# Three of four memory projections moved from behind a branch to the start of the kernel

## The chip, the cores and the metric

The kernel runs on one core of a Trainium2 chip. The metric is the device time of one launch in microseconds (us), the median of the timed runs. The engines named here are TensorE (PE in the profile, with PEld for its weight loads), VectorE (DVE), ScalarE (ACT), GpSimd (POOL) and SyncE (SP), whose queue issues most loads.

## The reference

Two transformer blocks run one after the other on 256 tokens of width 2048, in float32. The parts that matter here:

```
h  = concat(meta_tokens, x)                  # 16 + 256 rows
xn = rms_norm(h, norm1_g); proj = xn @ w_in  # first block, its first step
...
h  = h + peer(rms_norm(h))                   # experts: gelu(u_i . x), then sum of w_i * v_i over chosen i
h  = rms_norm(h, normf_g)
# second block: deltanet branch beside attention over a memory of 256 rows
mem_n = rms_norm(mem, mem_norm_g)
kv = mem_n @ w_kv                            # 2048 x 2048: 1024 columns of keys, 1024 of values
k  = rms_norm(heads of kv[:, :1024], kn_g);  v = kv[:, 1024:]
xa = softmax(q . k / 16) @ v                 # 4 heads of 256
```

The memory, its weights and its gains are inputs. `kv` depends on nothing that the first block computes; its keys and values are used in the second block's attention.

## The kernel before

**Products.** All large products are done in split float32: each operand is written as hi + lo (`split_store`, lines 173 to 180: one ACT operation for hi, one on DVE for lo), and `mm3` issues three matmuls. Weights come in loads of 1 MB into one of four `raw` buffers (SP's queue), are split in two halves into one of four `hi`/`lo` buffers, and are multiplied at once. `proj_a` makes 256 rows by 512 columns of an output out of 2048 inputs: four loads, eight halves, 96 matmuls of 512 columns. `Background` (`bg`) holds generators of small work; each load's `tick` lets one of them go on by its rate, so that this work stands in program order among the matmuls.

**Order.** Up to line 906 the order of every engine's instructions is planned by the compiler's scheduler, which takes the earliest in program order among those that its model has ready. From there on (`manual_schedule`) TensorE's order is the program's; the other engines' is still planned. Each engine then runs its own list strictly in order, with semaphores between them.

**The opening.** SP loads `meta` and the two halves of `x` (1 MB each), then eight rows of gains (`prows`), then the weights of `w_in`. ACT sums squares, DVE makes the rates (`rstd_of`, `rsqrt`: 13 small operations), `along` spreads them over the tokens with TensorE, and 16 sets of transposes (three each, line 335) with `xs` and a split on DVE and ACT make `xh`, `xl`. Then the projections of `w_in` follow.

**The memory.** While the experts' first layer runs (`hidden`, 64 steps), `memory()` loads `mem_T` (2 MB) and `mem_2` (2 MB) in the background from step 30 on, splits the memory with its gain into `mh`, `ml` (16 splits), and makes the rates `mr` of its rows.

**The branch.** The experts that any token chose are listed on the chip. If there are more than 106 x 128 of them, a slower path inside `tc.If` does the work; with these inputs it is not taken. The branch is a point at which all engines meet, and the scheduler moves nothing across it. Behind it stand, in program order: `weigh` for five pairs of rows (four POOL gathers each, two of `gq` and two of `hq`, with two buffers each; DVE multiplies them, and the product is split into `wh`, `wl`, of which the pool `wt` holds seven), the four memory projections (keys, keys, values, values), the transposes of the normalised keys, and the stores of keys and values to `kmd` and `vmd` in DRAM on ACT's queue.

**The value stage.** 53 pairs of rows: for each row of 128 experts, one POOL gather brings 1 MB of value rows into `raw`, it is split, and `add_row` adds it with 24 matmuls into eight PSUM banks. The weights of a pair are fetched five pairs ahead in program order. The last `LP` = 6 pairs are done by halves of the columns, so that the norm of the first half (`norm3(0)`, nine steps) can go beside the second half's matmuls.

Of the kernel before, what the change touches and what calls it, by code (L numbers as in the profile page):

```python
# [74 lines left out]
def _build(tc, nc, V, S, T, G, ctx, I, out):  # L75
# [27 lines left out]
    WA, LP = 5, 6  # L103
# [3 lines left out]

    pn1 = ctx.enter_context(ExitStack())
    nw1 = pn1.enter_context(pool("norm1"))
    meta = nw1.tile([NM, D], F32, name="meta", bufs=1)  # L110
    nc.sync.dma_start(meta, I["meta_tokens"])
    h = hp.tile([128, 2, D], F32, name="h")
    for t in range(2):
        nc.sync.dma_start(h[:, t], I["x"][0, t * 128:(t + 1) * 128, :])

# [111 lines left out]
    def proj_a(w, r0, nk, c0, xh, xl, t0=0):  # L227

        a = [acc() for _ in range(2)]
        for kg in range(nk // 4):  # L230
            src = w[r0 + kg * 512:r0 + (kg + 1) * 512, c0:c0 + 512].rearrange("(k p) n -> p k n", p=128)
            for k0, hi, lo in stream(src, 4, 512):
# [94 lines left out]

    w_in = I["w_in"][0]
    xh, xl = x_tiles(NM + NT)
    toks = [(meta, NM, 0), (h[:, 0], 128, NM), (h[:, 1], 128, NM + 128)]  # L330
    rB = along(nw1, rstd_of(square_sums(toks, nw1.tile([128, D], F32, name="junk")), D, [128, 3]), toks)
    for k in range(KT):
        p = (acc, ptp, acc, pmm)[k % 4]()
        for x, n, o in toks:
            T.transpose(p[:, o:o + n], chunk(x, k), ident[:n, :n])
        xs = nw1.tile([128, NM + NT], F32, name="xs", bufs=3)
        V.tensor_mul(xs, p[:, :NM + NT], rB)
        split_store(xh[:, k], xl[:, k], xs, pcol(N1, k))
# [547 lines left out]

    kmd = tc.dram_tile([128, 8, 256], F32, name="kmd")
    vmd = tc.dram_tile([128, 2, 1024], F32, name="vmd")
    def memory():

        ss = me.tile([128, 2, 4], F32, name="ssq")
        for hf in range(2):
            raw = load(I["mem_T"][:, hf * 8:hf * 8 + 8], [8, NT])
            for k in range(8):
                split_store(mh[:, hf * 8 + k], ml[:, hf * 8 + k], raw[:, k], pcol(MG, hf * 8 + k))
                yield
        for t in range(2):
            x = load(I["mem_2"][0, t * 128:(t + 1) * 128, :], [D])
            for q in range(4):
                S.activation(acc(), x[:, q * 512:(q + 1) * 512], AF.Square, accum_out=ss[:, t, q:q + 1])  # L900
            yield
        s1 = me.tile([128, 2], F32, name="ssr")
        V.tensor_reduce(s1, ss, axis=AX.X, op=OP.add)
        V.tensor_copy(mr, rstd_of(s1, D, [128, 2]))
        yield
# [868 lines left out]
```

## Time and profile before

| | |
|---|---|
| timed runs | 3509.72 us median of 3 (3509.1 to 3510.99) |
| the profiled execution | 3497.31 us, span 3495.4 us, granted clock 0.996 |
| PE busy | 3426.1 us, 98% of the span |
| DVE, ACT, POOL busy | 2386.8, 1626.7, 1031.5 us |
| DMA | 662.30 MB, 189 GB/s over the span |

A time in the timeline counts from the span's start. An engine's idle time in a stretch is the stretch less its busy time. In a timeline row, the brackets give how long the engine stood idle before the instruction and what released it. SPq and ACTq are the queues on which these engines issue DMAs. The opening is the stretch from 0 to about 28 us, the branch lies at about 1913 to 1919 us, the memory projections behind it go on to about 2024 us, and the value stage from there to about 2620 us.

### The profile page before, as it was taken

The page shows a single profiled execution, that of the slowest core. Times are in us where ns is not written, and L with a number is a line of the kernel's source. Part 1 is how long each engine was busy: PE and PEld are TensorE (multiplying, and loading weights), DVE is VectorE, ACT ScalarE, POOL GpSimd, SP SyncE. Part 2 cuts the span into 40 slices and gives each one's busy share as a digit, 9 for nine tenths or more (in the row PEclk, how much of TensorE's full clock was granted, in tenths as well). Part 3 has the DMA queues.
Part 4 walks back from the last instruction along what each step waited for, and adds up shares of the span by engine and source line. Part 5 has one row for each costly group of instructions (what it writes and reads, how often), then busy time and mean ns, then how long its engine had stood idle before and what let it go on. Part 6 is the DMA issues. An engine that isn't in the chain of part 4 may idle for free. (4 is left out here: it accounts for less than half of the span.)

```text
span 3495.4 us, 54464 instructions
## 1 busy us (share of the span) xinstructions
PE 3426.1 (98%) x21754; PEld 3080.0 (88%) x21754; DVE 2386.8 (68%) x4376; ACT 1626.7 (47%) x2148; POOL 1031.5 (30%) x660
## 2 busy tenths in 40 slices
PE   8999999999999999999998999999999999999999
PEld 7988899888889999999998788877778899999987
DVE  6975569977658997666453655544457788888775
ACT  6444443446455444444443544443347545444443
POOL 0000000000003888888810556666620000000000
PEclk9999999999999999999999999999999999999999
DMA  5544445667675676778764877666665444454443
GB/s 164 169 148 142 145 133 176 214 217 257 224 237 173 180 205 191 208 210 241 205 206 140 283 255 242 238 216 216 217 204 173 145 150 152 161 166 152 156 157 109
DMA packets 347976, 662.30 MB, mean 189 GB/s; under 512 B 56047, under 2 KB 205781, under 8 KB 318002
## 3 DMA queue, kind: packets, MB, share of 16 engines
q1 hardware_dynamic: 256962, 472.68, 40.5%
q0 software_dynamic: 71328, 165.08, 16.5%
q10 hardware_dynamic: 19424, 20.98, 1.7%
q8 instruction: 173, 2.83, 0.3%
q14 instruction: 89, 0.73, 0.1%
HBM read 620.47 MB, written 38.19 MB: 188 GB/s over the span
## 5 line engine op out<-in xcount | busy, mean ns | idle before, releaser
L176 ACT CAST hi<-raw 128x1024 fp32r<-128x1024 f32 x1093 | 1145.3, 1049 | 1549.9 <-PE acc L208 532.1
L177 DVE TENSOR_TENSOR lo<-raw,hi 128x1024 fp32r<-128x1024 f32 x1093 | 1330.4, 1222 | 711.7 <-ACT hi L176 706.3
L839 POOL DMA_INDIRECT table<-gts,idx x256 | 573.7, 2241 | 134.1 <-issue 75.3
L206 PE MATMUL acc<-xh,hi 128*128 128x256 f32 (+1 forms) x2048 | 604.2, 295 | 0.7 <-DVE hg L431 0.7
L206 PE MATMUL mm<-xh,hi 128*128 128x256 f32 x2064 | 586.2, 284 | 0.8 <-DVE fit L1017 0.8
L208 PE MATMUL acc<-xh,lo 128*128 128x256 f32 (+1 forms) x2048 | 586.1, 286 | 0.0
L207 PE MATMUL acc<-xl,hi 128*128 128x256 f32 (+1 forms) x2048 | 585.7, 286 | 0.0
L207 PE MATMUL mm<-xl,hi 128*128 128x256 f32 x2064 | 583.9, 283 | 0.0
L208 PE MATMUL mm<-xh,lo 128*128 128x256 f32 x2064 | 583.8, 283 | 0.0
L206 PEld LDWEIGHTS mm<-xh,hi 128*128 128x128 f32 x2064 | 394.9, 191 | 0.9 <-issue 0.8
L207 PEld LDWEIGHTS mm<-xl,hi 128*128 128x128 f32 x2064 | 395.0, 191 | 0.1
L208 PEld LDWEIGHTS mm<-xh,lo 128*128 128x128 f32 x2064 | 394.9, 191 | 0.0
L206 PEld LDWEIGHTS acc<-xh,hi 128*128 128x128 f32 x2048 | 389.7, 190 | 5.4 <-issue 4.9
L207 PEld LDWEIGHTS acc<-xl,hi 128*128 128x128 f32 x2048 | 390.0, 190 | 1.4 <-issue 1.0
L208 PEld LDWEIGHTS acc<-xh,lo 128*128 128x128 f32 x2048 | 389.1, 190 | 1.3 <-issue 1.2
L350 POOL DMA_DIRECT2D table<-zero x16 | 18.0, 1126 | 953.0 <-DVE zero L348 953.0
L206 PE MATMUL acc<-hi,xh 128*128 128x512 f32 x704 | 280.3, 409 | 0.0
L207 PE MATMUL acc<-lo,xh 128*128 128x512 f32 x704 | 278.2, 395 | 0.0
L208 PE MATMUL acc<-hi,xl 128*128 128x512 f32 x704 | 277.7, 394 | 0.0
L739 POOL DMA_INDIRECT gq<-table,ig x106 | 148.9, 1405 | 268.2 <-SPq L1137 153.1
L440 DVE SCALAR_TENSOR_TENSOR h<-hg,cw,h 128x256 f32<-128x256 f32 x480 | 203.4, 478 | 0.0
L207 PE MATMUL acc<-lo,wh 128*128 128x512 f32 x424 | 167.7, 395 | 16.9 <-DVE lo L177 16.9
(547 smaller groups left out, 5630.0 us busy)
## 6 DMA issues: line engine op xcount, KB each, us to landing
raw<-in_peer_u_dram SPq DMA_DIRECT2D x128, 1024.0 KB, 5.1
raw<-in_w_in_dram SPq DMA_DIRECT2D x112, 1024.0 KB, 5.0
raw<-in_dn_w_in_dram SPq DMA_DIRECT2D x88, 1024.0 KB, 4.9
raw<-in_w_out_dram SPq DMA_DIRECT2D x48, 1024.0 KB, 5.0
raw<-in_w_gla_out_dram SPq DMA_DIRECT2D x16, 1024.0 KB, 4.9
table<-zero POOLq DMA_DIRECT2D x16, 1024.0 KB
raw<-in_w_conv_out_dram SPq DMA_DIRECT2D x16, 1024.0 KB, 4.9
raw<-in_peer_wq_dram SPq DMA_DIRECT2D x16, 1024.0 KB, 5.3
```

The lines of the kernel that those rows point to most:

```text
L176: S.copy(hi, src)
L177: V.tensor_sub(lo, src, hi)
L206: T.matmul(o, lhsT=lh, rhs=rh, start=start, stop=False)
L207: T.matmul(o, lhsT=lh, rhs=rl, start=False, stop=False)
L208: T.matmul(o, lhsT=ll, rhs=rh, start=False, stop=stop)
L350: nc.gpsimd.dma_start(table[:128 * 128 * NT].rearrange("(q p a b) o -> q p a (b o)", q=16, p=128, b=128)[q], z[:, None, :].to_broadcast([1 ...
L440: V.scalar_tensor_tensor(ca[:, f], hg[:, f - f0, j:j + NT], w, ca[:, f], op0=OP.mult, op1=OP.add)
L739: G.indirect_dma_start(out=dst, out_offset=None, in_=rows, in_offset=bass.IndirectOffsetOnAxis(ap=ids.bitcast(U32), axis=0))
L839: d = G.indirect_dma_start(out=table, out_offset=bass.IndirectOffsetOnAxis(ap=idx[:, i, s:s + 1].bitcast(U32), axis=0), in_=gts[:, i, s:s ...
```

## The change

- `memory()` moves up in the program and runs twice: at the opening, at once and not in the background, with its own tiles, and, as before, beside the experts' first layer. A hook in it places the loads of `meta` and `x` behind the second load of `mem_T`.
- The first norm becomes a generator, `norm1()`, in the background of three memory projections at the rate 1.6; its transposes use the banks of `ptp` and `pmm` by turns.
- These three projections, the keys of column block 1 and both blocks of values, now stand before the projections of `w_in`. The transposes of the keys of block 1 come between the two of values.
- Behind the branch the keys of block 0 are left, and their transposes follow at once. Their first 512 rows of weights are loaded and split before the branch, into tiles of their own (`begun`).
- `mem_keys` stores the transposed keys in two parts with one buffer (`kms`), where there was one part.
- The pool `wt` has six buffers instead of seven, `LP` is 5 instead of 6, and `norm3(0)` goes on at 1.4 instead of 1.0 a tick.

```diff
-    WA, LP = 5, 6
+    WA, LP = 5, 5
...
+    h = hp.tile([128, 2, D], F32, name="h")
     pn1 = ctx.enter_context(ExitStack())
     nw1 = pn1.enter_context(pool("norm1"))
     meta = nw1.tile([NM, D], F32, name="meta", bufs=1)
-    nc.sync.dma_start(meta, I["meta_tokens"])
-    h = hp.tile([128, 2, D], F32, name="h")
-    for t in range(2):
-        nc.sync.dma_start(h[:, t], I["x"][0, t * 128:(t + 1) * 128, :])
...
-    def proj_a(w, r0, nk, c0, xh, xl, t0=0):
+    def proj_a(w, r0, nk, c0, xh, xl, t0=0, begun=None):
...
-            for k0, hi, lo in stream(src, 4, 512):
+            for k0, hi, lo in begun if begun and kg == 0 else stream(src, 4, 512):
...
+    def memory(hook=None):
+        ss = me.tile([128, 2, 4], F32, name="ssq")
+        for hf in range(2):
+            raw = load(I["mem_T"][:, hf * 8:hf * 8 + 8], [8, NT])
+            if hook is not None:
+                hook(hf)
+            for k in range(8):
+                split_store(mh[:, hf * 8 + k], ml[:, hf * 8 + k], raw[:, k], pcol(MG, hf * 8 + k))
+                yield
...
-    rB = along(nw1, rstd_of(square_sums(toks, nw1.tile([128, D], F32, name="junk")), D, [128, 3]), toks)
-    for k in range(KT):
-        p = (acc, ptp, acc, pmm)[k % 4]()
...
+    def norm1():
+        rs = rstd_of(square_sums(toks, nw1.tile([128, D], F32, name="junk")), D, [128, 3])
+        yield
+        rB = along(nw1, rs, toks)
+        yield
+        for k in range(KT):
+            p = (ptp, pmm)[k % 2]()
+            for x, n, o in toks:
+                T.transpose(p[:, o:o + n], chunk(x, k), ident[:n, :n])
+            xs = nw1.tile([128, NM + NT], F32, name="xs", bufs=3)
+            V.tensor_mul(xs, p[:, :NM + NT], rB)
+            split_store(xh[:, k], xl[:, k], xs, pcol(N1, k))
+            yield
+
+    def first_loads(hf):
+        if hf == 0:
+            return
+        nc.sync.dma_start(meta, I["meta_tokens"])
+        for t in range(2):
+            nc.sync.dma_start(h[:, t], I["x"][0, t * 128:(t + 1) * 128, :])
+
+    def mem_keys(wk, cb, mh, ml, mr, begun=None):
+        ks = []
+        for t, a in enumerate(proj_a(wkv, 0, KT, cb * 512, mh, ml, begun=begun)):
+            ks.append(wk.tile([128, 512], F32, name="kn", bufs=2))
+            heads_norm(wk, a, ks[-1], mr[:, t:t + 1])
+        yield
+        for hd in range(2):
+            km = wk.tile([128, 2, 256], F32, name="kms", bufs=1)
+            for f in range(2):
+                p = ptp()
+                for t in range(2):
+                    T.transpose(p[:, t * 128:(t + 1) * 128], chunk(ks[t], hd * 2 + f), ident)
+                S.activation(km[:, f], p[:, :256], AF.Copy, scale=xag[:, 2 + f:3 + f])
+            nc.scalar.dma_start(kmd[:, cb * 4 + hd * 2:cb * 4 + hd * 2 + 2], km)
+
+    with pool("mem0", side="right") as me, pool("kvw0", side="right") as kvw:
+        mh, ml, mr = mem_tiles()
+        for _ in memory(first_loads):
+            pass
+        bg.add(norm1(), 1.6)
+        keys = mem_keys(kvw, 1, mh, ml, mr)
+        next(keys)
+        for cb in range(2):
+            for t, a in enumerate(proj_a(wkv, 0, KT, 1024 + cb * 512, mh, ml)):
+                vm2 = kvw.tile([128, 512], F32, name="vn", bufs=2)
+                S.activation(vm2, a, AF.Copy, scale=mr[:, t:t + 1])
+                nc.scalar.dma_start(vmd[:, t, cb * 512:(cb + 1) * 512], vm2)
+            if cb == 0:
+                for _ in keys:
+                    pass
+        bg.drain()
     pn1.close()
...
-    wp = pwt.enter_context(pool("wt", bufs=7))
+    wp = pwt.enter_context(pool("wt", bufs=6))
...
+    be = pbe.enter_context(pool("begun", side="right"))
+    raw = load(wkv[0:512, 0:512].rearrange("(k p) n -> p k n", p=128), [4, 512])
+    begun = []
+    for f in range(2):
+        hi, lo = (be.tile([128, 2, 512], F32R, name=f"{n}{f}") for n in ("bh", "bl"))
+        split_store(hi, lo, raw[:, f * 2:f * 2 + 2])
+        begun.append((f * 2, hi, lo))
     with tc.If(nc.values_load(ids["n"][0:1, 0:1]) > NS * 128):
...
     ws = [weigh(e2, wp, ww) for e2 in range(WA)]
     with pool("kvw", side="right") as kvw:
-        ks = []
-        for cb in range(2):
-            for t, a in enumerate(proj_a(wkv, 0, KT, cb * 512, mh, ml)):
-                ks.append(kvw.tile([128, 512], F32, name="kn", bufs=4))
-                heads_norm(kvw, a, ks[-1], mr[:, t:t + 1])
-        for cb in range(2):
-            for t, a in enumerate(proj_a(wkv, 0, KT, 1024 + cb * 512, mh, ml)):
-                vm2 = kvw.tile([128, 512], F32, name="vn")
-                S.activation(vm2, a, AF.Copy, scale=mr[:, t:t + 1])
-                nc.scalar.dma_start(vmd[:, t, cb * 512:(cb + 1) * 512], vm2)
-            km = kvw.tile([128, 4, 256], F32, name="kms")
-            for _ in heads_T(ks[cb * 2:cb * 2 + 2], km, 0, 2):
-                pass
-            nc.scalar.dma_start(kmd[:, cb * 4:cb * 4 + 4], km)
+        for _ in mem_keys(kvw, 0, mh, ml, mr, begun):
+            pass
+    pbe.close()
     pme.close()
...
         if hf == 1:
-            bg.add(norm3(0), 1.0)
+            bg.add(norm3(0), 1.4)

```

## Rows read from the trace of the kernel before

**Rows 1.** The page's part 1: busy us, share of the span, instructions

```profile
PE 3426.1 (98%) x21754; PEld 3080.0 (88%) x21754; DVE 2386.8 (68%) x4376; ACT 1626.7 (47%) x2148; POOL 1031.5 (30%) x660
```

**Rows 2.** The windows: from:to, length, busy PE, PEld, DVE, ACT, POOL, clock, DMA, GB/s

```profile
0.00:28.30 28.30, 14.54 (x56) 9.26 (x57) 19.87 (x69) 16.20 (x22) 3.58 (x12) 1.00 0.90 311
...
1912.90:1925.20 12.30, 0.02 (x2) 0.00 (x1) 0.71 (x2) 1.73 (x3) 4.44 (x5) 0.58 0.50 169
...
1925.20:1931.70 6.50, 6.04 (x13) 4.42 (x14) 4.70 (x4) 3.02 (x4) 4.58 (x4) 0.50 1.04 399
...
1931.70:2024.50 92.80, 89.81 (x391) 71.88 (x390) 55.73 (x105) 49.57 (x66) 43.83 (x38) 1.00 0.77 264
...
2024.50:2282.00 257.50, 257.50 (x1137) 213.21 (x1136) 144.25 (x140) 113.19 (x120) 169.84 (x143) 1.00 0.71 245
...
2282.00:2540.00 258.00, 241.14 (x1034) 193.50 (x1033) 125.80 (x130) 101.97 (x108) 164.50 (x125) 0.99 0.63 218
```

**Rows 3.** The opening in order of time: start, us, engine, line, operation, idle before

```profile
1.19 0.88 SPq L114 DMA_DIRECT2D h<-in_x_dram  x2
...
4.72 0.42 SPq L155 DMA_DIRECT2D prows<-in_norm_g_dram  x1
...
6.20 1.11 PE L335 MATMUL acc<-ident,h 128*128 128x128 f32 x4 [1.84 <-DMA h<-in_x_dram]
...
9.31 1.12 PE L335 MATMUL acc<-ident,h 128*128 128x128 f32 x4 [2.00 <-DMA h<-in_x_dram]
```

**Rows 4.** Groups by line of the first 100 us: count, busy us, mean ns

```profile
L176 ACT CAST hi<-raw 128x1024 fp32r<-128x1024 f32 x21 | 21.3, 1044 | 9.0 <-DMA raw<-in_w_in_dram 4.2 <-PE acc L207 2.3 <-issue 1.9
...
L180 DVE SCALAR_TENSOR_TENSOR xl<-xs,prm,xh 128x272 fp32r<-128x272 f32 x16 | 7.5, 492 | 0.2 <-ACT xh L179 0.2
...
L337 DVE TENSOR_TENSOR xs<-acc,rB 128x272 f32<-128x272 f32 x8 | 3.5, 431 | 0.0
...
L263 ACT ACTIVATE junk<-h 128x2048 f32<-128x2048 f32 x2 | 3.8, 1912 | 0.3 <-DMA h<-in_x_dram 0.3
```

**Rows 5.** The branch in order of time, queues of ACT and SP, and TensorE

```profile
1914.35 0.37 ACTq L758 DMA_DIRECT2D hid<-gel  x1
...
1918.97 68.40 SPq L185 DMA_DIRECT2D raw<-in_mem_w_kv_dram  x15
...
1925.20 0.80 PE L206 MATMUL acc<-hi,mh 128*128 128x512 f32 x1 [12.28 <-ACT hi L176]
```

**Rows 6.** Groups by line behind the branch, 1912 to 2025 us

```profile
L303 ACT ACTIVATE kn<-acc,mr 128x512 f32<-128x512 f32 x4 | 2.7, 679 | 0.0
...
L250 DVE SCALAR_TENSOR_TENSOR rs_r<-rs_u,rs_r 128x2 f32<-128x2 f32 x12 | 1.8, 161 | 0.1
```

**Rows 7.** The tile vn, a 256 KB store on ACT's queue

```profile
DMA to landing us min/median/max: 6.2/6.2/6.2
```

**Rows 8.** ACT in order of time, first key projection's norm

```profile
1950.03 0.68 ACT L303 ACTIVATE kn<-acc,mr 128x512 f32<-128x512 f32 x1
...
1969.19 0.91 ACT L311 ACTIVATE kn<-kn,rs_r 128x256 f32<-128x256 f32 x2 [0.35 <-DVE rs_r L250]
```

**Rows 9.** POOL in order of time behind the branch

```profile
1919.54 1.01 POOL L739 DMA_INDIRECT gq<-table,ig  x1 [153.11 <-SPq L1137]
...
1977.19 0.95 POOL L739 DMA_INDIRECT hq<-hid,ih  x1 [0.30 <-issue]
```

**Rows 10.** POOL in the value stage's second half, in order of time

```profile
2297.78 1.69 POOL L739 DMA_INDIRECT gq<-table,ig  x1 [2.55 <-DVE hq L1058]
...
2301.51 1.96 POOL L739 DMA_INDIRECT raw<-in_peer_v_dram,ih  x1 [0.30 <-issue]
...
2309.74 1.69 POOL L739 DMA_INDIRECT gq<-table,ig  x1 [2.52 <-DVE hq L1058]
```

**Rows 11.** DVE in the value stage's second half, in order of time

```profile
2300.30 2.35 DVE L177 TENSOR_TENSOR lo<-raw,hi 128x1024 fp32r<-128x1024 f32 x2
...
2308.78 0.69 DVE L1058 TENSOR_TENSOR hq<-hq,gq 128x512 f32<-128x512 f32 x1 [6.13 <-DMA hq<-hid,ih]
```

More of the change, by code (lines that the diff above doesn't have):

```diff
@@ L325, in x_tiles, with mem_tiles @@
         return a, b
+    kmd = tc.dram_tile([128, 8, 256], F32, name="kmd")
+    vmd = tc.dram_tile([128, 2, 1024], F32, name="vmd")
+    def mem_tiles():
+        return [me.tile([128, KT, NT], F32R, name=n) for n in ("mh", "ml")] + [me.tile([128, 2], F32, name="mr")]
+    def memory(hook=None):
[8 more added lines that the diff above has]
+        for t in range(2):
+            x = load(I["mem_2"][0, t * 128:(t + 1) * 128, :], [D])
+            for q in range(4):
+                S.activation(acc(), x[:, q * 512:(q + 1) * 512], AF.Square, accum_out=ss[:, t, q:q + 1])
+            yield
+        s1 = me.tile([128, 2], F32, name="ssr")
+        V.tensor_reduce(s1, ss, axis=AX.X, op=OP.add)
+        V.tensor_copy(mr, rstd_of(s1, D, [128, 2]))
+        yield
+    wkv = I["mem_w_kv_2"][0]
     w_in = I["w_in"][0]
@@ L330, in _build @@
     toks = [(meta, NM, 0), (h[:, 0], 128, NM), (h[:, 1], 128, NM + 128)]
-    rB = along(nw1, rstd_of(square_sums(toks, nw1.tile([128, D], F32, name="junk")), D, [128, 3]), toks)
-    for k in range(KT):
-        p = (acc, ptp, acc, pmm)[k % 4]()
[L334 to L338, printed above, removed]
+    def norm1():
[10 more added lines that the diff above has]
+            split_store(xh[:, k], xl[:, k], xs, pcol(N1, k))
+            yield
@@ new lines, in first_loads @@
+    def first_loads(hf):
[9 more added lines that the diff above has]
+            heads_norm(wk, a, ks[-1], mr[:, t:t + 1])
+        yield
+        for hd in range(2):
+            km = wk.tile([128, 2, 256], F32, name="kms", bufs=1)
+            for f in range(2):
+                p = ptp()
+                for t in range(2):
+                    T.transpose(p[:, t * 128:(t + 1) * 128], chunk(ks[t], hd * 2 + f), ident)
+                S.activation(km[:, f], p[:, :256], AF.Copy, scale=xag[:, 2 + f:3 + f])
+            nc.scalar.dma_start(kmd[:, cb * 4 + hd * 2:cb * 4 + hd * 2 + 2], km)
@@ L884, in choose @@
         yield from compact(steps[0][:, :128])
[L887 to L905, printed above, removed]
     ctx.enter_context(tc.manual_schedule(engines={mybir.EngineType.PE}))
@@ L1120, in _build @@
             me = pme.enter_context(pool("mem", side="right"))
-            mh = me.tile([128, KT, NT], F32R, name="mh")
-            ml = me.tile([128, KT, NT], F32R, name="ml")
-            mr = me.tile([128, 2], F32, name="mr")
+            mh, ml, mr = mem_tiles()
             bg.add(memory(), 0.75)
@@ L1133, in _build @@
     pwt = ctx.enter_context(ExitStack())
-    wp = pwt.enter_context(pool("wt", bufs=7))
+    wp = pwt.enter_context(pool("wt", bufs=6))
     pww = pwt.enter_context(ExitStack())
     ww = pww.enter_context(pool("wtw", bufs=2))
+    pbe = ctx.enter_context(ExitStack())
+    be = pbe.enter_context(pool("begun", side="right"))
[5 more added lines that the diff above has]
+        begun.append((f * 2, hi, lo))
     with tc.If(nc.values_load(ids["n"][0:1, 0:1]) > NS * 128):
```

1 line of the change is left out of this document (removed).

## The prediction

> **What bounds the kernel now.** I read the page's busy times first: TensorE is busy 98% of the span [rows 1], so only its 69 us without work can be given back, and the windows say where those are. 13.8 us lie ahead of the first projection (28.30 less 14.54 busy), 12.3 us behind the branch, 3.5 us in the rest of the four memory projections, none in the first half of the expert-value stage (2024.5 to 2282), 16.9 us in its second half [rows 2]. The change touches all of these places. I then read the opening in order of time [rows 3], the few lines that set its pace [rows 4], the branch [rows 5], the end of a key projection [rows 6 to 8], and POOL and DVE in the value stage [rows 9 to 11].
>
> The same matmuls run before and after, so the sum is made over TensorE's idle time in three places. One proj_a is 96 matmuls of 512 columns. In the dense half of the value stage 1137 of these take 257.5 us, 0.2265 us each [rows 2], so a projection is 21.7 us and three of them move 65 us of work, with eight of the 16 key transposes, from behind the branch to the opening. That alone is worth nothing.
>
> **The opening.** It adds one run of memory(): two 1 MB loads of mem_T, two of mem_2, 16 splits, eight squares; and it puts these loads ahead of the first weights on SP's queue. What must land before the first projection can start is then: mem_T (2 MB), meta (0.13), x (2), mem_2 (2), the first weights (1). Before, it was meta, x and one load of weights. The two x loads, issued from 1.19 on, landed when the transposes that waited for them began, 6.20 and 9.31: 5.0 us for the first, 3.1 for each MB behind it [rows 3]. The eight gain rows now go first, at about half a microsecond each on SP (the sixth of them was issued at 4.72, the first behind the x loads' issue at 2.07 [rows 3]), so mem_T starts at about 4.7 and its first half is there at 9.7. Then 0.4 for meta and six more MB at 3.1: the first weights land at 28.7, the split gives its first half 1.04 us later [rows 4], and the first memory matmul starts at about 29.8. The w_in projection that it replaces started at 28.3. So the wait for the first norm is not covered by the projections: they wait for more bytes than the norm did.
>
> What counts is how much of the norm's TensorE work fits into that wait. Before, all of it did: 14.54 us, of which 0.7 are the gain rows' transposes, 1.7 the broadcast of the rates, and 12.1 the 16 sets of transposes, 0.76 each [rows 2]. Now x is complete only at 19.4; the squares take 1.91 us for each half [rows 4], the rates and their broadcast took some 5.5 us behind the last square (DVE's small operations, then 1.7 us on TensorE), so the rates are there at about 27. Four sets can go before that, since norm1() has four PSUM banks; after it a set is released every 0.92 us (xs 0.43 and xl 0.49 on DVE [rows 4]), five more by 31. Nine sets and the rest are 9.2 us: idle 29.8 - 9.2 = 20.6, and 0.9 for waiting on the first two low parts, 21.5 against 13.8: **+8 us**. From below: if all 14.5 us fit and the loads come at 2.7 us per MB (the rate at the branch, 399 GB/s [rows 2]), 26.5 + 0.9 - 14.5 = 12.9, a gain of 1; from above: no set before the projections, 31 - 2.4 - 13.8 = +15. I take the sum by the x rows, the nearest transfers. The seven sets left go beside 65 us of matmuls. The 16 splits (about 0.5 us on each of ACT and DVE, by xl) run from 9.7 to 18 while both engines wait for x; they hide, and so do the squares of mem_2. The loads that now come later (wa, wab, the w_in weights) have 65 us of matmuls ahead of them. One 256 KB store of kms stands between the two halves of the keys, since kms has one buffer: ACT waits for its landing, 2 to 6 us, which the four split tiles (10.9 us of matmuls) cover; 0, at most +4.
>
> **The branch.** TensorE's last expert matmul is at 1912.9, the last activation's store is issued at 1914.35, SP's first load behind the branch at 1918.97, and TensorE starts at 1925.20, after the load (5 us) and a split [rows 5]. With the first weights split before the branch the load and the split drop out: TensorE should start at about 1919.3, and 12.3 becomes 6.4. The granted clock was 0.50 until 1931.7 [rows 2], which is 1.2 GHz; the engine had stood 12 us. It will have stood 6, so I keep the 3.1 us that this cost (bounds 0 and 3.1). The next weights land at 1924 while the ready ones last to 1927: no second wait.
>
> But the projection left here is the key projection, and TensorE's order is the program's from peer_wq on: its eight transposes come straight behind it. Before, the keys' norms had a later projection to hide in. The projection ends at 1919.3 + 21.7 + 3.1 = 1944.1. The chain behind it, with free engines, is scaling (0.68), square, reduction (about as long each), 13 small DVE operations at 0.16 and what lies between them, two scalings, the second token tile behind the first: an estimate of 7.5 us [rows 6]. Half the heads' transposes and evacuations take 1.5. Then the single kms buffer is stored, and the other half's evacuation waits for that to land: 6.2 us for the store of the same size on that queue in this stretch [rows 7]. Only then are the two PSUM banks free in which the value stage's first matmul writes. That is 1960.4: 16.3 us, of which 2.3 are transposes. Idle 6.4 + 14.0 = 20.4, against 12.3 + 3.5 = 15.8 before: **+5 us**. Bounds: a store of 2 us and nothing else, +0.6; the chain as slow as it ran before, where DVE had gathered weights in between (1950.03 to 1970.1 instead of 7.5 [rows 8]), +17.
>
> **The value stage.** Each pair of rows needs six gathers from POOL: four for the weights, two for the values. In the second half TensorE is short because of them: mul(hq) waits on DVE for its gather (6.13 us), the low parts of the values stand behind it on DVE, and the next gq waits for that product (2.52 us) [rows 10, 11]. That loop is 11.96 us (2297.78 to 2309.74) where a pair of rows is 10.87. Before, POOL had 112 us between the branch and the stage, of which it used 59 to fetch nine pairs of weights (36 gathers, 1919.54 to 1978.1, 1.63 each [rows 9]); that lead held 257.5 us, 24 pairs, then 16.9 us were lost in 258 [rows 2], 0.8 a pair. Now it has 41, which is 25 gathers: five pairs of weights and the first four rows, and no more. wt has six buffers instead of seven, so the lead cannot grow far either. If the time that a lead holds goes with its size (five of nine), the lateness begins after 13 pairs instead of 24: 11 pairs at 0.8, **+8 us**. From above: late from the first pair, 43 pairs at 1.09 less 16.9, +30. From below: the gathers come in another order and are never late, -17. I take the proportion; nothing here shows the stage started with a short lead.
>
> A gather takes 0.95 us, but 1.96 where it begins beside a pair of low-part subtractions (2301.51 against 2300.30 [rows 10, 11]). The Trainium skill (SBUF — State Buffer, Who interferes with whom) has a two-input tensor_tensor contend only with POOL's reads, and infers that it leaves descriptor generation alone; taken so, six gathers with their gaps and the 2.5 us wait would be 10.0 us, under a pair's 10.87, and the 16.9 us could not be there. The rows disagree with the inference, and the same two instructions meet after the change.
>
> LP 6 to 5 and norm3's 1.4: one pair more goes by whole rows (two gathers less on POOL), and norm3's nine steps find 10 ticks at 1.4 where they had 12 at 1.0. I take 0; if the half's five pairs no longer cover it, a step of norm, 2 us.
>
> **Sum.** 8 + 5 + 8 = +21 us on the profiled execution's 3497.3 (span 3495.4 and 1.9 around it), 3518. The median of the timed runs lies 12.4 above it; the same step from 3509.7 gives 3531, which I forecast.
>
> **Rivals.**
> (1) POOL is behind from the first pair: its static order fetches ahead more than 41 us allow, TensorE waits at the start, and a loop of 11.96 never catches up with 10.87. For it: once late, the trace shows no recovery until the gathers end. Against: the stage starts late itself. 8 + 5 + 30: 3553.
> (2) The other side: with a short lead POOL gathers each pair's gq and hq together and no gq waits for a landing. Its loop is then six gathers and gaps, 9.5 us, and the 16.9 us go. For it: POOL's order is planned anew, from a start with few gathers done. Against: the order in the stage now has gq a pair ahead of hq [rows 10]. With the opening at +3 and the branch at +1: 3497. It decides as soon as that loop is under 10.87 and the other two cost less than 17.
> (3) The whole norm does fit into the wait for the weights (opening +1), the store of kms lands in 2 us (branch +1), and the value stage is as before: 3512, no change.
>
> **How the numbers follow.** Forecast 0.40 (3517 to 3545), rival 1 0.25, rival 2 0.17, rival 3 0.18. A change under 0.2% (7 us) can't be told from none here. Slower 0.40 + 0.25, faster 0.17, same 0.18. The range leaves out the lower half of rival 2 and the upper part of rival 1: 3499 to 3555.
>
> **What would show it.** Right: the first memory matmul at 28 to 31 us and TensorE idle about 21 us up to there; TensorE starting 6.4 us behind the last expert matmul; a gap of some 14 us between the key projection and the first value matmul, ended by kms; waits of the low parts for hq before the stage's middle. Wrong: a first matmul before 26 us, a gap under 8 us, or a value stage whose late half is shorter than 258 us.

## The result and the profile after

The changed kernel takes 3560.14 us (median of four runs, 3551.56 to 3561.66) against 3510.06 for the kernel before on the same chip: a ratio of 1.015, interval 1.0129 to 1.017. I had forecast 3531 within 3499 to 3555. The side was right; the 21 us forecast were less than half of the 50 that came, and the time lies above the range. The profiled execution has a span of 3559.9 us against 3495.4.

The page's part 1 of the changed kernel (busy us, share, instructions), to be read against [rows 1]:

```profile
PE 3438.3 (97%) x21754; PEld 3079.6 (87%) x21754; DVE 2387.1 (67%) x4407; ACT 1637.6 (46%) x2180; POOL 1040.7 (29%) x658
```

The matmuls are the same in number. TensorE is busy 12.2 us longer and without work 52.3 us longer (3559.9 less 3438.3, against 69.3). The windows of the changed kernel say where, in the columns of [rows 2]:

```profile
0.00:29.50 29.50, 2.38 (x8) 1.22 (x8) 12.74 (x54) 19.48 (x41) 2.51 (x10) 1.00 0.83 312
...
1992.40:2003.20 10.80, 0.06 (x2) 0.05 (x1) 3.14 (x3) 2.72 (x3) 0.00 (x0) 0.60 0.09 28
2003.20:2008.20 5.00, 5.00 (x12) 3.94 (x13) 0.00 (x0) 0.01 (x1) 3.46 (x4) 0.51 0.77 270
...
2026.40:2050.40 24.00, 4.89 (x17) 2.90 (x17) 10.11 (x38) 10.12 (x18) 17.83 (x22) 0.62 0.77 267
2050.40:2612.00 561.60, 520.02 (x2209) 415.06 (x2208) 267.71 (x277) 216.54 (x231) 363.27 (x278) 0.99 0.63 214
```

Idle ahead of the first projection: 27.1 us, where [rows 2] have 13.8, so +13.4. Behind the branch 10.7 and in the gap ahead of the value stage 19.1: 29.9 against 15.7, +14.1. In the value stage 41.6 against 16.9, +24.7. These three make 52.2.

The other 12.2 us, by which TensorE is busy longer, lie in the value stage too. The whole stage, from its first matmul to the end of its last, before and after:

```profile
2023.93:2629.21 605.28, 585.92 (x2558) 478.44 (x2559) 317.22 (x317) 254.91 (x279) 358.38 (x291) 1.00 0.66 226
2049.64:2694.04 644.40, 600.33 (x2558) 480.96 (x2559) 312.35 (x322) 253.97 (x279) 384.53 (x299) 0.99 0.63 212
```

The same 2558 matmuls count as busy for 14.4 us more, so the stage is 39.1 us longer and not 24.7: a matmul that starts a little late or runs slower still counts as busy. The stage starts 25.7 us later, and these two make the span's 64.5 but for 0.3.

**The opening**, in order of time on ACT, DVE and TensorE (start, us, engine, line, what, idle before it):

```profile
19.65 1.91 ACT L259 ACTIVATE junk<-h 128x2048 f32<-128x2048 f32 x1
23.59 0.58 ACT L342 ACTIVATE acc<-raw 128x512 f32<-128x512 f32 x1
28.48 3.87 ACT L172 CAST hi<-raw 128x1024 fp32r<-128x1024 f32 x4
28.88 0.16 DVE L251 TENSOR_SCALAR rs_v<-ssn 128x3 f32<-128x3 f32 x1
29.57 1.22 PE L202 MATMUL acc<-hi,mh 128*128 128x512 f32 x2 [9.99 <-ACT hi L172]
35.74 0.60 DVE L292 TENSOR_SCALAR dg<-ident,rs_r 16x16 f32<-16x16 f32 x3
```

The first memory matmul starts at 29.57, as forecast (29.8), but not for the reason forecast: the split of its weights (28.48) stands on ACT behind the last of mem_2's eight squares. The norm's rates have their squares by 23.7 and wait on DVE until 28.88, behind the same squares and the row rates, and are done at 35.74. So two sets of transposes went ahead of the projections, not nine.

**Branch and key norms** on ACT, TensorE and DVE:

```profile
1994.40 1.04 ACT L172 CAST bh<-raw 128x1024 fp32r<-128x1024 f32 x1 [0.57 <-ACT gel L828]
1998.10 1.04 ACT L172 CAST bh<-raw 128x1024 fp32r<-128x1024 f32 x1 [2.65 <-SPq L1193]
2003.18 0.76 PE L202 MATMUL acc<-bh,mh 128*128 128x512 f32 x1 [10.74 <-DVEq L1193]
2039.56 0.69 DVE L1108 TENSOR_TENSOR hq<-hq,gq 128x512 f32<-128x512 f32 x1 [7.27 <-DMA hq<-hid,ih]
2042.90 0.47 PE L389 MATMUL tp<-ident,kn 128*128 128x128 f32 x1 [14.86 <-ACT kn L307]
2049.11 0.84 ACT L390 ACTIVATE kms<-tp,xag 128x256 f32<-128x256 f32 x2 [1.84 <-DMA kmd<-kms]
2049.64 0.80 PE L202 MATMUL tp<-hi,wh 128*128 128x512 f32 x1 [3.53 <-issue]
```

"Ahead of the branch" the two splits stand behind the last gelu, and the second starts 2.65 us after the first has ended, released by SP's queue at the branch's line (L1193). Its low part ends at 2000.4, and the engines are past the branch only then: SP's first load behind it goes out at 2003.11, 10.7 us behind the last expert matmul, where it was 6.1 before. TensorE waits 10.7 us instead of 12.3. Then it waits 14.9 us for the scaled keys. Half of that is one DVE instruction: the first pairs' mul(hq) stands between the steps of the key norm and waits 7.27 us for its gather. The last wait, 3.5 us, has no releaser in the profile ("issue"); that it is the evacuation into kms is read from ACT's order, where this evacuation starts at 2049.11, after the store has landed.

**The value stage.** The waits of DVE and POOL from 2050.4 to 2612 (total, times, longest), and one cycle of it on DVE and POOL, to be read against [rows 10, 11]:

```profile
DVE hq L1108 <- DMA hq<-hid,ih: 281.9, 46, 7.7
...
POOL gq L810 <- DVE hq L1108: 117.1, 43, 4.0
```

```profile
2309.35 0.69 DVE L1108 TENSOR_TENSOR hq<-hq,gq 128x512 f32<-128x512 f32 x1 [7.63 <-DMA hq<-hid,ih]
2309.96 2.35 DVE L173 TENSOR_TENSOR lo<-raw,hi 128x1024 fp32r<-128x1024 f32 x2
2310.31 1.69 POOL L810 DMA_INDIRECT gq<-table,ig  x1 [4.02 <-DVE hq L1108]
2312.23 0.68 DVE L173 TENSOR_TENSOR wl<-hq,wh 128x512 fp32r<-128x512 f32 x1
2312.30 1.43 POOL L810 DMA_INDIRECT gq<-table,ig  x1 [0.30 <-issue]
2312.83 2.35 DVE L173 TENSOR_TENSOR lo<-raw,hi 128x1024 fp32r<-128x1024 f32 x2
2314.04 1.96 POOL L810 DMA_INDIRECT raw<-in_peer_v_dram,ih  x1 [0.30 <-DVE lo L173]
2316.30 0.94 POOL L810 DMA_INDIRECT hq<-hid,ih  x1 [0.30 <-issue]
2317.55 0.95 POOL L810 DMA_INDIRECT hq<-hid,ih  x1 [0.30 <-issue]
...
2321.34 0.69 DVE L1108 TENSOR_TENSOR hq<-hq,gq 128x512 f32<-128x512 f32 x1 [6.16 <-DMA hq<-hid,ih]
```

mul(hq) releases two gq, a raw follows, then two hq, and their landing releases the next mul(hq): 11.99 us from 2309.35 to 2321.34, where a pair's matmuls take 10.87. The changed kernel is in this cycle from the mul(hq) at 2088.78 on, the tenth of 53 and 39 us into the stage. Every eighth pair takes 13.2 to 13.5 us there, since hq lands some 1.4 us later (as it did ahead of 2309.35); why it does is not shown. The kernel before runs the same order of instructions without loss for 257 us; its cycle at 2117 us, DVE and POOL, and the mul(hq) with which it goes late:

```profile
2116.90 0.69 DVE L1058 TENSOR_TENSOR hq<-hq,gq 128x512 f32<-128x512 f32 x1 [0.57 <-DMA hq<-hid,ih]
2117.83 1.29 DVE L177 TENSOR_TENSOR lo<-raw,hi 128x1024 fp32r<-128x1024 f32 x1 [0.24 <-ACT hi L176]
2117.86 0.94 POOL L739 DMA_INDIRECT gq<-table,ig  x1 [0.71 <-DVE hq L1058]
2119.11 0.94 POOL L739 DMA_INDIRECT gq<-table,ig  x1 [0.31 <-issue]
2120.36 0.94 POOL L739 DMA_INDIRECT raw<-in_peer_v_dram,ih  x1 [0.30 <-issue]
...
2127.67 0.69 DVE L1058 TENSOR_TENSOR hq<-hq,gq 128x512 f32<-128x512 f32 x1 [0.45 <-DMA hq<-hid,ih]
...
2284.84 0.69 DVE L1058 TENSOR_TENSOR hq<-hq,gq 128x512 f32<-128x512 f32 x1 [5.28 <-DMA hq<-hid,ih]
```

The difference between the two cycles is three durations. Where mul(hq) comes late, all four high parts are ready, DVE's subtractions stand in a row behind it, and gq, gq and raw take 1.69, 1.43 and 1.96 us beside them instead of 0.94 each: 2.26 us. Without these the late cycle would be 9.7.

### The profile page after: what moved, and what is told of

Read it like the earlier page. It is cut to its first block, busy times and chain, and to the rows that moved or that the text cites. A ratio compares the mean times of both kernels' runs of the same rounds, so it can differ in the third digit from the quotient of the medians.

```text
span 3559.9 us, 54523 instructions
## 1 busy us (share of the span) xinstructions
PE 3438.3 (97%) x21754; PEld 3079.6 (87%) x21754; DVE 2387.1 (67%) x4407; ACT 1637.6 (46%) x2180; POOL 1040.7 (29%) x658
## 3 DMA queue, kind: packets, MB, share of 16 engines
q0 software_dynamic: 71040, 165.08, 16.3%
## 5 line engine op out<-in xcount | busy, mean ns | idle before, releaser
L1108 DVE TENSOR_TENSOR hq<-hq,gq 128x512 f32<-128x512 f32 x53 | 36.7, 692 | 295.8 <-DMA hq<-hid,ih 293.1
```

What stands on the lines that cost most here:

```text
L1108: V.tensor_mul(hq, hq, gq)
```

## The experiments

My theory had four parts: the value stage is held by that loop, not by sizes or POOL's throughput; the loop is too long only because of the slow gathers; the opening lost by the order of the norm's rates; the key norm by having nothing behind it. Each kernel was run beside the kernel before, whose own runs spread from 3476 to 3524 us (medians of the four jobs 3502.6 to 3509.7), so the changes are read in the traces first.

**1. The three sizes alone**, in the kernel before.

```diff
-    WA, LP = 5, 6
+    WA, LP = 5, 5
-    wp = pwt.enter_context(pool("wt", bufs=7))
+    wp = pwt.enter_context(pool("wt", bufs=6))
-            bg.add(norm3(0), 1.0)
+            bg.add(norm3(0), 1.4)
```

> The kernel before with only the three sizes of the change: wt with six buffers, LP 5, norm3 at 1.4 a tick. Theory (the value stage is late because it starts with a short lead of gathers and with the key gap ahead of it, not because of the sizes): as before, 3506 to 3514 us, and the value stage's idle TensorE time is within 6 us of what the kernel before shows. Rival (one weight buffer less is what makes the stage late from its beginning): 3528 to 3540, with TensorE idle 20 to 30 us more in the value stage and nothing changed up to there.

Measured: 3509.09 us, ratio 0.9992 (0.9963 to 1.0022). From 2024.5 to 2586 TensorE is idle 23.8 us, where the kernel before shows 16.9 in its profile: 6.9, a little more than I allowed, and within the spread of that kernel's runs. The sizes don't explain the lateness. What differs between the two profiles is when it begins: the pairs of 12 us start at 2187 us here and at 2272 in the kernel before, and the stage is 617.8 us long instead of 605.3, in a run of 3511.6 us instead of 3497.3.

**2. x ahead of mem_T**, in the changed kernel.

```diff
-        for _ in memory(first_loads):
+        first_loads(1)
+        for _ in memory():
```

> The changed kernel with the loads of meta and x issued ahead of mem_T's instead of between its halves. Theory (the opening's idle time is norm1's rates coming late: x lands at 16 to 19 us, and its squares and rates stand among mem_2's on ACT and DVE): x lands by 11, the rates are ready before the first weights, most of the sixteen sets of transposes go ahead of the first projection, which still starts at 28 to 31 us; idle TensorE time ahead of it falls from 27 to 15 to 20, and the run is 7 to 12 us under the changed kernel, 3548 to 3553. Rival (DVE's splits of mem_T, which stand ahead of the norm in program order, hold it anyway): no set more goes ahead, within 3 us of the changed kernel.

Measured: 3550.22 us (3548.04 to 3555.69), ratio 1.0127 (1.0101 to 1.0152). The median is 9.9 us under the changed kernel's, as the theory said, though the intervals of the two ratios overlap. The mechanism is not the theory's: idle up to 29.5 us is 25.9 instead of 27.1. x was there by 12.71 and its squares were done at 15.1, yet the rates were still computed from 26.94 to 34.1. So it was not the late x that kept the norm out of the wait; the rates stood behind mem_2's squares in the engines' orders. The profiled execution's 6.0 us are spread over opening, key norms and value stage.

**3 and 4. Three buffers for gq and hq**, in the changed kernel (which has no room for the weights split ahead then, so without them) and in the kernel before.

```diff
-    ww = pww.enter_context(pool("wtw", bufs=2))
+    ww = pww.enter_context(pool("wtw", bufs=3))
```

> The changed kernel with three buffers instead of two for gq and hq, and without the weights split ahead of the branch (the memory has no room for both). Theory (the value stage is a loop: mul(hq) on DVE waits for hq's landing, the values' low parts stand behind it, and the next gq waits for that product because there are only two buffers): the gathers get a pair further ahead, the waits of mul(hq) fall from some 6 us to under 1, TensorE's idle time in the value stage falls from 42 us to under 12, and the run is 3520 to 3535. Rival (POOL's own work, six gathers at 1 to 2 us and the starts between them, is the 12 us a pair): the period stays at 12 us, 3555 to 3565.

> The kernel before with three buffers instead of two for gq and hq, nothing else. Theory (the same loop holds the second half of its value stage): the 16.9 us without work there go, the run is 3485 to 3497, below both kernels. Rival (POOL's own work is the bound as soon as its lead is spent): 3506 to 3513, and the second half still has 15 us or more without work.

Measured: 3546.48 us, ratio 1.0122 (1.0096 to 1.0147), and 3500.32, ratio 0.9989 (0.9958 to 1.002). Both miss. The value stage's idle time falls from 41.6 to 19.8 us in the first (2058 to 2612, where its stage starts at 2058.1); in the second its 19.5 us (2024.5 to 2586) are no less than before. The order of POOL's rows fits this: with three buffers gq goes two pairs ahead of hq instead of one, and the mul(hq) that releases it still needs the two hq gathered last. A buffer more puts off the late cycle (to about 2220 in the changed kernel) and leaves the loop closed.

**5 and 6. hq gathered ahead of gq**, in the kernel before and in the changed kernel; only the order of the four gathers changes.

```diff
             for e in range(2):
                 k = e2 * 2 + e
-                fetch(gq[:, e], ...)
-                fetch(hq[:, e], hid, ids["h"][:, k:k + 1])
+                last = fetch(hq[:, e], hid, ids["h"][:, k:k + 1])
+            with tc.issue_after(last.ins):
+                for e in range(2):
+                    k = e2 * 2 + e
+                    fetch(gq[:, e], ...)
```

> The kernel before with one thing changed: of each pair's four weight gathers POOL issues the two hq ahead of the two gq (buffers as they were). Then mul(hq) needs nothing that POOL gathered since the last mul(hq). Theory (a loop mul(hq), two gq, raw, two hq, their landing, next mul(hq) of 10.8 to 12 us sets the pace as soon as the lead is spent): the loop is gone, the second half of the value stage loses under 4 us instead of 16.9, every run lies at 3472 to 3484, below the median of the kernel before by 20 to 30. Rival (POOL's six gathers a pair are as such too slow): the value stage loses 15 us or more and the time stays at 3495 to 3510.

> The changed kernel with the same one thing: hq gathered ahead of gq. Theory (the same loop, here from the stage's second or third cycle on because the lead was never built up): of the 42 us without work in the value stage 30 or more go, 3522 to 3532. What is left over the kernel before is then the opening and the branch with the key norms, +13 and +14. Rival (POOL's throughput, with a short lead): the period stays at 12 us a pair, 3550 to 3562.

Measured: 3471.31 us (3470.33 to 3473.04), ratio 0.9896 (0.9874 to 0.9919): it beats both kernels, and the spread of 30 us is gone. The changed kernel so mended takes 3505.46, ratio 0.9998 (0.998 to 1.0016), 55 less than without. Both gained more than I expected: most runs of the first lie under 3472, and the second is 17 us under its 3522. The second half of the first's value stage, and the whole stage of the first and of the second:

```profile
2282.00:2540.00 258.00, 258.00 (x1140) 213.67 (x1139) 146.47 (x140) 111.44 (x119) 157.83 (x138) 1.00 0.68 240
```

```profile
2022.37:2603.64 581.27, 578.77 (x2558) 478.76 (x2559) 326.05 (x317) 254.38 (x279) 331.51 (x295) 1.00 0.67 237
2046.84:2639.75 592.91, 590.04 (x2558) 478.58 (x2559) 312.23 (x322) 254.28 (x279) 363.04 (x298) 0.99 0.66 230
```

The half that lost 16.9 us [rows 2] loses nothing, and in the changed kernel's stage 2.9 us are idle. But that stage is still 11.6 us longer than the other, nearly all of it counted as busy. One cycle of it on DVE and POOL:

```profile
2305.45 0.69 DVE L1111 TENSOR_TENSOR hq<-hq,gq 128x512 f32<-128x512 f32 x1 [5.22 <-DMA gq<-table,ig]
2308.15 1.69 POOL L810 DMA_INDIRECT hq<-hid,ih  x1 [2.09 <-DVE wl L173]
2310.15 1.97 POOL L810 DMA_INDIRECT hq<-hid,ih  x1 [0.30 <-issue]
...
2316.48 0.69 DVE L1111 TENSOR_TENSOR hq<-hq,gq 128x512 f32<-128x512 f32 x1 [5.19 <-DMA gq<-table,ig]
```

One part of the expectation was wrong: mul(hq) does wait for gathers issued since the last one, now gq's (5.2 us). The order takes the raw gather out of the loop and puts the product's split (wl) in. Two gathers, now hq's, are still slow beside the subtractions, and the loop is 11.0 us, a little longer than a pair's 10.87. The mended kernel before stays clear of it, with pairs of 10.9. TensorE's busy time in the whole changed kernel falls by 12.2 us as well, to 3426.1, so the late cycle had also made matmuls slower, not only waits.

**7. Is it the form of the subtraction?** In the changed kernel.

```diff
-            V.tensor_sub(lo, src, hi)
+            V.scalar_tensor_tensor(lo, src, 1.0, hi.bitcast(F32), op0=OP.mult, op1=OP.subtract)
```

> The changed kernel with every low part that is split without a scale made by scalar_tensor_tensor (times 1.0, less hi) instead of tensor_tensor subtraction; the values are the same. The disputed cost is the gather's 1.69 to 1.96 us beside a subtraction against 0.95 alone. Theory (it is the form tensor_tensor of DVE that slows POOL's descriptors): gathers fall to 0.95 throughout, the loop of a pair falls from 12.0 to under 10.8, the lateness in the value stage heals, 3520 to 3535. Rival (any DVE operation beside it slows them, or the slow gathers are not what holds the loop): the gathers keep 1.4 us or more on average beside the low parts and the period stays at 11.5 to 12.5; 3550 to 3575, the more if this form takes longer.

Measured: 3558.61 us, ratio 1.0143 (1.0121 to 1.0166). The rival holds. The groups of gathers from 2100 to 2540 us (count, busy us, mean ns, idle before), in this kernel:

```profile
L810 POOL DMA_INDIRECT gq<-table,ig x72 | 112.2, 1558 | 111.5 <-DVE hq L1108 100.5 <-issue 11.0
L810 POOL DMA_INDIRECT raw<-in_peer_v_dram,ih x72 | 104.6, 1453 | 21.9 <-issue 21.0 <-DVE lo L173 0.9
```

In the changed kernel these means are 1559 and 1454. The other form takes as long and slows them as much.

**8. No low parts of the values**, in the changed kernel: the subtractions are taken away, and nothing else of the loop.

```diff
-            for hf, hi, lo in halved(v_row(e2 * 2 + e), 2, 1024):
-                add_row(a[hf], e, ws[e2], hi, lo, e2 == 0 and e == 0, False)
+            for hf, hi in halves(v_row(e2 * 2 + e)):
+                add_row(a[hf], e, ws[e2], hi, hi, e2 == 0 and e == 0, False)
```

> The changed kernel, in which the low parts of the expert values that are read by whole rows are left out: DVE makes none of them, and TensorE runs the same matmuls with the high part in their place. Gathers, their order and their buffers are those of the changed kernel. Theory (the loop of a pair is 12.0 us instead of some 10 because its two gq and its raw run at 1.69, 1.43 and 1.96 us beside DVE's subtractions instead of 0.95): the gathers fall to 0.95, the loop to under 10.5, the value stage's idle time from 42 us to under 8, 3515 to 3528. Rival (the gathers are slow for another reason, or the landing of hq is what holds the loop): gathers at 1.4 us and more on average, and the period at 11.5 to 12.

Measured: 3497.98 us (3495.7 to 3500.3), ratio 0.9967 (0.9957 to 0.9976), lower than either theory said: the theory counted idle time alone, and TensorE's busy time falls too, by 17.4 us (3438.3 to 3420.9). The gathers from 2100 to 2540 us and the value stage's window:

```profile
L810 POOL DMA_INDIRECT raw<-in_peer_v_dram,ih x81 | 76.5, 944 | 26.4 <-ACT hi L1131 14.2 <-issue 12.2
L810 POOL DMA_INDIRECT gq<-table,ig x80 | 75.6, 945 | 88.6 <-DVE hq L1108 76.4 <-issue 12.2
```

```profile
2050.40:2612.00 561.60, 559.10 (x2458) 462.61 (x2457) 89.23 (x118) 243.21 (x262) 282.37 (x297) 1.00 0.70 235
```

The gathers take 0.94 to 0.95 us on average, the same loop with the same short lead and the same buffers keeps up with TensorE, and 2.5 us are idle. The second part of the theory is shown: the loop is too long only beside the subtractions.

**9. Two projections behind the branch**, two in the opening, the key transposes last; no weights split ahead.

```diff
+        keys = mem_keys(kvw, 0, mh, ml, mr)
+        next(keys)
+        mem_values(kvw, 1, mh, ml, mr)
+        for _ in keys:
+            pass
```

> The changed kernel with two projections in the opening (second keys, first values; norm1 beside them at 2.4 a tick) and two behind the branch: first keys, then second values, the keys' transposes behind the latter; no weights split ahead of the branch. Theory (the key norms' chain costs 14 us because no projection stands behind it, and the value stage is late because POOL has a projection less of lead): the gap of 19 us ahead of the value stage shrinks to under 5, POOL gains 22 us of lead, TensorE's idle time in the value stage is 5 to 15 us less than 42; 3530 to 3545. Rival (neither depends on where the projections stand): 3555 to 3565, with the gap at 15 us or more.

Measured: 3543.97 us, ratio 1.0103 (1.0081 to 1.0126), as expected; the gap not quite. The wait for scaled keys is gone, but 10.6 us (1.7 and 8.9) remain for ACT's evacuation into kms, whose one buffer is free only when its store has landed. The value stage's idle time is 34.8 (2041.5 to 2603): 22 us of lead bought 6.8.

**10. The norm ahead of the memory**, with hq ahead of gq.

```diff
-        for _ in memory(first_loads):
+        first_loads(1)
+        steps = norm1()
+        for _ in range(11):
+            next(steps)
+        for _ in memory():
             pass
-        bg.add(norm1(), 1.6)
+        bg.add(steps, 1.6)
```

> Opening only, on top of hq ahead of gq (3505.5): meta and x are loaded first, and norm1's rates, their broadcast and nine of its sixteen sets are emitted ahead of the memory's splits and squares instead of beside the first projection. Theory (the nine sets of my sum did not go into the wait because the rates stood behind mem_2's squares and row rates on ACT and DVE, not because x came late): ten or more us of norm1 go ahead of the first memory matmul, idle TensorE time up to there falls from 27 to 15 to 21 us, 3495 to 3502. Rival (ACT and DVE have no room: mem_T's sixteen splits and the squares then come later and put off the first weights' split by as much): the first matmul moves from 29.6 to 34 or later, idle time stays at 24 or more, 3503 to 3510.

Measured: 3501.12 us (3499.57 to 3505.38), ratio 0.9984 (0.9973 to 0.9994), 4.3 under experiment 6, whose ratio's interval overlaps this one. The opening's window:

```profile
0.00:29.50 29.50, 9.05 (x33) 5.93 (x34) 17.93 (x77) 21.99 (x46) 2.50 (x10) 1.00 0.81 312
```

The first memory matmul starts at 28.96 and 20.5 us are idle up to 29.5 instead of 27.1. That is about the 20.6 of my sum, reached once the order lets the norm go: eight sets go ahead, not nine, and somewhat under eight us of the norm fit, not the ten expected here.

**11. No weights split ahead, and two buffers for kms**, with hq ahead of gq.

```diff
-    begun = []
...
-            km = wk.tile([128, 2, 256], F32, name="kms", bufs=1)
+            km = wk.tile([128, 2, 256], F32, name="kms", bufs=2)
```

> Two edits that are read in two stretches, on top of hq ahead of gq (3505.5). Branch: no weights split ahead of it. Theory: TensorE waits 12 to 13.5 us there instead of 10.4, so the split ahead is worth 2 to 3, not the 5.9 of my sum. Rival: 15 or more. Key norms: two buffers for kms instead of one. Theory: the 5.2 us that the value stage's first matmul waited for the store of kms fall to under 1, the 13.0 us for the scaled keys stay. Rival (the banks or POOL's first gathers hold it as well): 4 us or more remain. Together 3502 to 3506.

Measured: 3506.21 us, ratio 0.999 (0.9975 to 1.0004). SP's first load behind the branch and TensorE's waits, in order of time:

```profile
1997.38 2.46 SPq L181 DMA_DIRECT2D raw<-in_mem_w_kv_dram  x4
2003.64 0.80 PE L202 MATMUL acc<-hi,mh 128*128 128x512 f32 x1 [11.56 <-ACT hi L172]
2038.12 0.48 PE L389 MATMUL tp<-ident,kn 128*128 128x128 f32 x1 [9.51 <-ACT kn L307]
2043.32 1.11 PE L389 MATMUL tp<-ident,kn 128*128 128x128 f32 x4 [3.50 <-ACT kms L390]
```

12.0 us at the branch (11.56, and 0.46 for the first low part) against 10.4 in experiment 6: the split ahead is worth 1.6, less than I expected even here. Without it SP's first load goes out 5.3 us behind the last expert matmul (it ends at 1992.07), so the split had put the branch off by about 5 us. The waits for the scaled keys, expected to stay at 13.0, fell to 9.8; mul(hq) between the norm's steps waits 2.7 us and not 4.8, some two of these three. The value stage's first matmul no longer waits; but ACT's order had a small step of a later stage (128x24 numbers, with their load) ahead of the evacuation, so 3.5 of the 5.2 us came back. The total shows nothing of it.

**12. All losses mended**: experiments 6, 9, 10 and the buffers of 11 together.

> The change with each of its losses mended: hq ahead of gq; norm1's nine steps ahead of the memory in the opening; two projections in the opening and two behind the branch (first keys, second values, then the keys' transposes); two buffers for kms; no weights split ahead. Theory (the losses are separate and add up): from 3505.5, the opening gives 4 as measured alone, the key gap of 18 us falls to under 4 and gives 14, two projections behind the branch leave the value stage dense: 3484 to 3490. It stays above the kernel before with hq ahead of gq (3471.3), since the opening still waits 20 us instead of 13.5 and the slow clock behind it stays. Rival (with the gather loop mended, moving projections out is worth something): 3471 or less. If the losses do not add: 3496 or more.

Measured: 3481.66 us (3479.43 to 3488.31), ratio 0.9954 (0.9932 to 0.9976). That is 2.3 under the range expected, but the parts are not those of the sum. In the profile the value stage starts 12.3 us earlier than in experiment 6 (2034.5 against 2046.8), not 18, and it is itself 10.7 us shorter (582.3 us, pairs of 10.9), which the sum did not have: with two projections behind the branch it stays out of the loop of 11.0. That the total comes near the sum is luck. It stays 10 us above experiment 5, with 20.7 us idle in the opening (29.5 less 8.81 busy) against 13.5 there.

## Why the prediction was wrong, point by point

In the two profiles the value stage starts 25.7 us later and is 39.1 us longer. The medians have 50 in all, since the kernel before's profiled execution lies 12.8 us under its median. With hq ahead of gq neither kernel has the cycle of 12 us, so experiments 5 and 6 divide the 50: that cycle costs the kernel before 3509.3 - 3471.3 = 38 us and the changed one 3560.1 - 3505.5 = 55 (medians of different jobs), 17 of the change. The other 34 are, in the profiles of these two, a value stage that starts 24.5 us later, for the opening, the branch and the key norms, and that is 11.6 us longer, by the loop of 11.0.

**The value stage, +8 forecast, +39.1 in the profile (24.7 of it idle) and, as an estimate from these, 17 + 11.6, some 28 in the medians.** The step that failed is "if the time that a lead holds goes with its size, the lateness begins after 13 pairs instead of 24". A lead does not run down at 0.8 us a pair. The stage has two cycles: 10.8 us where gathers run clear of the subtractions, and 12.0 where they stand in them; whoever falls into the second stays there until the gathers end, since it is longer than a pair's matmuls. The changed kernel starts short enough to fall in at once; the kernel before falls in after one late landing (hq lands 4.3 us behind its last gather where a pair earlier it took 2.7, and mul(hq) waits 5.28 us at 2284.84 where the two waits before it were 3.8 and 3.6). That is rival 1, with its place. That its time (3553) comes near is in part luck: its 30 us for the stage were 39 in the profile, its opening and branch were too small as well, and the median of the kernel before hid 12.8 of the difference. I had read the loop of 11.96 correctly and still put a proportion in its place. Rival 2's mechanism, gathers ordered so that the loop is short, is real and worth 38 us in the kernel before, but the change doesn't make it.

I had also taken the 1.96 us of [rows 10] against the Trainium skill (SBUF — State Buffer, Who interferes with whom), which infers that a two-input tensor_tensor leaves descriptor generation alone. Experiment 8 decides for the rows: gq and raw take 0.94 to 0.95 us without the subtractions, 1.45 to 1.56 on average with them.

**The opening, +8 forecast, +13.4 measured.** The first matmul at 29.57 against 29.8 is luck. In experiment 2 the same loads precede the first weights, and their split starts at 26.55 and the first matmul at 27.63; so the bytes were priced too high, and mem_2's squares on ACT made up for it. The step that failed is "nine sets and the rest are 9.2 us": TensorE did 2.4 us of work there. I let the rates be ready at 27 by x's landing, and counted mem_2's squares as hidden. They hide for TensorE and not for the norm, whose rates stand behind them; experiment 2 (x earlier, nothing gained) and experiment 10 (rates earlier, 6.7 us of idle time gained) separate the two. And the rates and their broadcast did not take "some 5.5 us behind the last square" in the kernel before: its last square ends at 11.35, and the broadcast rates are there at 21.08, 9.7 us later. DVE and ACT there:

```profile
15.86 1.22 DVE L177 TENSOR_TENSOR lo<-raw,hi 128x1024 fp32r<-128x1024 f32 x1 [1.44 <-ACT hi L176]
17.00 0.15 DVE L250 SCALAR_TENSOR_TENSOR rs_r<-rs_u,rs_r 128x3 f32<-128x3 f32 x1
20.69 0.39 ACT L298 COPY rB<-mm 128x272 f32<-128x272 f32 x1 [1.14 <-PE mm L297]
```

A weight's low part already stood ahead of the rates' last step. In the changed kernel it is 18.9 us (23.7 to 42.6).

**Branch and key norms, +5 forecast, +14.1 measured.** Two steps failed. "TensorE should start at about 1919.3", 6.4 us behind the last expert matmul: it waits 10.7. I had left the end of the branch where it was, but the split stands ahead of it, waits itself for ACT's last gelu, and puts it off; experiment 11 gives 1.6 us for it where I had 5.9. And "an estimate of 7.5 us" for the key chain "with free engines": it takes 14.9, as DVE is held by mul(hq) for 7.27 in between. The size was right and "free" was not: less the wait of mul(hq), 7.6 us are left here and 7.8 in experiment 6 (12.6 less 4.83). The wait for kms, 6.2 in my sum, is 3.5 here and 5.2 in experiment 6: right in kind. The terms named for this gap, 7.5, 1.5 and 6.2, add to 15.2 us, where I wrote 16.3; the other 1.1 has no row.

**Sizes and profile.** LP, wt and norm3 at nothing: upheld (experiment 1). That the timed runs lie 12.4 us above the profiled execution I had carried over as a constant; I put it down to the moment at which the late cycle sets in, which differs from run to run. What speaks for it is that the runs of experiment 5 lie within 2.7 us of each other, and that experiment 1's profile, 14.3 us longer than the kernel before's, has it set in 85 us earlier; the moment in an unprofiled run was not seen.

## What to carry to other kernels

Where an engine's wait and another's buffer close a loop, work out the loop's length in both of its states, with the durations that each has beside the other engine's work; if one state is longer than the time it has, a short lead can fall into it for good, as here, where one more buffer only put it off. What mended it was a shorter loop, here by the order of four gathers. Compare the length of a whole stage too, and not only the idle time in it: here 14 of 39 us, and once nearly all of 11.6, counted as busy. And work that hides from the bottleneck may still stand ahead of what the bottleneck waits for: follow the order on each engine, not only its free time.

## What the hardware showed that I had not expected

A gather that begins while a DVE subtraction runs seems to stand until that instruction ends (or the next, if it begins at the very end), and then to take some 0.85 us. In the late cycle above, the first lo ends at about 2311.13 (the pair of 2.35 from 2309.96), wl at 2312.9 and the second pair at 2315.18; the gathers beside them end at 2312.00, 2313.73 and 2316.00, 0.8 to 0.9 later. From 2100 to 2540 us in the changed kernel all 108 gathers that begin with no DVE instruction running take 0.94 to 0.95 us, and all 108 that begin in a subtraction 1.43 to 1.97. A gather that starts within some 0.04 us of the subtraction is not held, and the subtraction is longer instead (1.29 for 1.23 us at 2117.83); so it is with all 56 such gathers of the kernel before and of experiment 5 from 2060 to 2540 us. scalar_tensor_tensor with both inputs in the same places does as tensor_tensor does. That it is a lock is argued from these ends; that the subtractions cause it, experiment 8 shows.
